# The first product of each key tile at distance 160, and the second gathered block begun one pair of heads at a time

## The chip, the cores and the metric

The kernel runs on one core of one Trainium2 chip, as one launch. The metric is the device time in microseconds (us) of that core. TensorE is called PE here, its weight loads PEld, VectorE DVE, ScalarE ACT, GpSimd POOL and SyncE SP; L199 is line 199 of the kernel before the change.

## The reference

One transformer layer on 512 tokens of width 2048, in float32:

```python
x = layer_norm(DN_ALPHA * x + hybrid_mixer(...))            # mLSTM and forgetting attention
x = layer_norm(DN_ALPHA * x + memory_cross_attention(...))
x = layer_norm(DN_ALPHA * x + peer_ffn(...))

def peer_ffn(x, w_pq, sub_keys, expert_u, expert_v):
    q = (x @ w_pq).reshape(B, S, 8, 2, 128)
    sc = jnp.einsum('bshpd,hpnd->bshpn', q, sub_keys)
    top_s, top_i = lax.top_k(sc, 16)                        # per head, on each of two halves of the key
    cand_s = top_s[..., 0, :, None] + top_s[..., 1, None, :]
    cand_i = top_i[..., 0, :, None] * 128 + top_i[..., 1, None, :]
    best_s, best_pos = lax.top_k(cand_s, 16)                # 16 of 256 pairs
    idx, g = take_along_axis(cand_i, best_pos), softmax(best_s)
    a = einsum('tkd,td->tk', expert_u[idx], x)              # 8 heads x 16 = 128 experts per token
    return einsum('tk,tkd->td', gelu(a) * g, expert_v[idx])
```

There are 16384 experts. The change touches the last of the three sublayers only, and what runs beside its beginning.

## The kernel before, in words

**Numbers.** A float32 weight is used as two halves that PE can multiply fast: `hi`, its value rounded (written by ACT, L194), and `lo`, the remainder (a subtraction on DVE, L199). The activations are split in the same way. A product of weights W and activations X is the sum of three: hi of W by hi of X, hi of W by lo of X, and lo of W by hi of X. Weights come in tiles of 1 MB (128 x 2048 numbers) by SP's DMA queue, are split into a ring of two tiles (`ring`, `shares`, L181), and are used by PE while the other ring tile is being filled. Each ring subtraction is one L199 row in the profile; the text calls it a tick.

**Blocks.** The 512 tokens are four blocks of 128. In the last sublayer blocks 0 and 1 are gathered: for each of the 128 expert places of a token, an indirect DMA on POOL's queue (L1062) fetches one row of the table `peer_u` for each of the 128 tokens, 1 MB in all, and DVE multiplies it by the token and sums (L1082, "u use"); after the gates have been applied, rows of `peer_v` are fetched and DVE adds them up (L1098, "v use"). The rows land in a pool of three buffers. Blocks 2 and 3 are dense: all 16384 experts are computed by PE, 128 key tiles of 128 experts. `next_a` (L1361) does the u part of one key tile: 16 pairs of products L1374 (hi by hi) and L1377 (hi of the weights by lo of X), then 16 products L1381 (lo by hi), 48 of 256 columns (the 256 tokens), which share a PSUM bank two tiles at a time and then go through a Gelu. `stage_o` does the v part: per tile 24 products of 512 columns (L1530, L1531, L1527).

**The choice of experts** (`Choice`, L930): PE projects the tokens to queries and multiplies by the keys (`run`, L1006) for two heads at a time, four groups; ACT copies the scores out (L1040); DVE finds the best 16 (`select`, L950, some 40 small instructions over L941 to L993). After the last group `soften` (L996) turns the scores into gates, and `indices` (L1044) makes the expert numbers, as one instruction each for all eight heads.

**Order of the work around the change.** The instructions of each engine run in the order in which a scheduler places them; the program's generators are advanced by hand. Block 0's gathers run beside the attention of the blocks after it and end at 2459.6 us. Block 1's hidden state is finished by `e1.norm`; then, in the pool `pick1`, the choice for block 1 (`cr`) is advanced step by step between the cross-attention of blocks 2 and 3 (`att`), their output projection (`res`, L789 and L270) and `e2.norm` (L802), which makes `X2`, the transposed and split activations of blocks 2 and 3. After it come, in this order: the choice for blocks 2 and 3 with 30 key tiles beside it ("top-k stage", some 2870 to 3150 us), then more key tiles while the dense gates are built (`gbuild`, to some 3440 us), a first round of v tiles without u tiles (to some 3775 us), and the main stage, in which a u tile and a v tile alternate (to some 4490 us); then the end (last sums and layer norm on DVE, then the output's DMA).

**Gathers** are paced by the ticks (`tick`, L1143): each adds `rate * cost * mult` to a credit; at 1.0 the next job's gather is issued behind that tick, and its use is put on DVE's queue `lag` ticks later. `add_jobs(1)` (L1140) puts block 1's 128 u and 128 v jobs on the list, when its choice has been made.

**Distances.** `shift` pools hold a few bytes so that the buffers after them start at another address. The "distance" of a product is the address of its moving operand (the activations) less that of its weights, modulo 256 bytes. For the key tiles it is 192 for all 16 slices of X2 before the change.

The function that makes X2 allocates its tiles from `pair(fpl, "X", 16)`: 16 tiles of 512 columns, each holding two slices, hi and lo apart.

Of the kernel before, what the change touches and what calls it, by code (L numbers as in the profile page):

```python
# [49 lines left out]
def build(tc, I, out):  # L50
    nc = tc.nc
    NC_ = PKEYS
    with ExitStack() as ctx:
# [36 lines left out]
        def parts(a, b, n):  # L90
            return [(a[:, i:i + n], b[:, i:i + n]) for i in range(0, 512, n)]
# [41 lines left out]
        iota = cp.tile([P, P], F32, tag="iota", name="iota")  # L133
        ei = [cp.tile([P, P], I32, tag=f"ei{t}", name=f"ei{t}") for t in range(2)]
        nc.gpsimd.iota(ei[0], pattern=[[1, P]], base=0, channel_multiplier=0)
# [13 lines left out]
        cols = cp.tile([P, 2, TB, 4], F32, tag="cols", name="cols")  # L149
        gg = [cp.tile([P, P], F32, tag=f"gg{t}", name=f"gg{t}") for t in range(2)]  # L150


# [622 lines left out]
        class Ends:  # L775
# [26 lines left out]
            def norm(self, i, o, alloc, dst, mid=None):  # L802
# [11 lines left out]
                for g in range(4):  # L814
# [8 lines left out]
                    for cc in range(nb):  # L823
# [15 lines left out]
                        a, l = alloc()  # L839
                        split(a, l, f)  # L840
                        o.extend(parts(a, l, w))
                        fs.append(f)
# [87 lines left out]
        class Choice:  # L930
# [74 lines left out]

            def run(self, X2, ld):  # L1006
                tp, nb = self.tp, self.nb
                for g in range(4):
# [21 lines left out]
                    for t in range(nb):  # L1030
# [10 lines left out]
                        self.select(t, 2 * g, sc)  # L1041
                self.soften()

# [16 lines left out]
        def gather(table, t, k, s):  # L1060
            rows = rows_tile("rows")
            i = nc.gpsimd.indirect_dma_start(out=rows, out_offset=None, in_=I[table],  # L1062
                                             in_offset=bass.IndirectOffsetOnAxis(ap=ei[t][:, k:k + 1], axis=0))
            pace(i, s)
            return rows
# [74 lines left out]
        def add_jobs(t):  # L1140
            jobs.extend((f, t, k) for f in (job_u, job_v) for k in range(NC_))

# [199 lines left out]
        while state["done"] < len(jobs):  # L1342
            raise RuntimeError(f"{len(jobs) - state['done']} jobs left")
        add_jobs(1)
        state["lag"] = 2
        set_rate(980.0)
        state["mult"] = 0.65
# [13 lines left out]
        def next_a(hold=None):  # L1361
# [7 lines left out]
            for uh, ul, o, w in shares(raw, 2.1, hold):  # L1369
# [8 lines left out]
                for kk in range(w // P):  # L1378
                    k = o // P + kk
                    sl = slice(kk * P, (kk + 1) * P)  # L1380
                    i = nc.tensor.matmul(bank, ul[:, sl], X2[k][0], start=False, stop=k == 15)  # L1381
            abank[1:] = [i]
# [77 lines left out]
        hs, g4 = {}, {}  # L1460
        state["mult"] = 0.86

# [203 lines left out]
```

## Time and profile before

| what | value |
|---|---|
| median of 3 runs | 4523.76 us (4520.47 to 4525.49) |
| the profiled execution | 4524.7 us |
| its span in the trace | 4523.0 us |
| mean granted PE clock | 0.992 |
| first gather of block 1 | 2869.84 us |
| last v use of block 1 ends | 4495.5 us |

The profiled execution's own time lies 1.7 us over its span and 0.9 us over the median. The span is that of the instructions in the trace; the times are of the device. On the page and in the answers of the trace, "PE busy (x)" is the time in which matmuls were under way and their number. Matmuls overlap one another, so the cost of one in a steady stream is the distance between the starts of two, not its own duration.

### The profile page before, as it was taken

Reading aid. Unit: us, or ns where it says so; the run is one execution under the profiler, and the core shown is the slowest. Engines: PE = TensorE matmul, PEld = TensorE weight load, DVE = VectorE, ACT = ScalarE, POOL = GpSimd, SP = SyncE. Lnnn points to the kernel's source line nnn. Section 1 sums busy time; section 2 is a strip of 40 time slices with the busy share of each in tenths; the row PEclk is TensorE's granted clock in tenths of the full one; section 3 lists DMA queues with packets and bytes.
Section 4 is the critical chain, followed back from the end, with each engine's and each line's share of the span. In section 5 each row is a group of like instructions: output and inputs, shape, how many; then the busy total and the mean of one; then the engine's idle time right before and its main releaser. Section 6 shows DMA issues by size and latency. Waiting matters only on the chain.

```text
span 4523.0 us, 65247 instructions
## 1 busy us (share of the span) xinstructions
PE 4414.1 (98%) x25702; PEld 3966.6 (88%) x25702; DVE 3739.9 (83%) x4326; ACT 2229.8 (49%) x3032; POOL 895.5 (20%) x631
## 2 busy tenths in 40 slices
PE   9999999999999999999999999898999999999998
PEld 8888888889888899999999778898998778999996
DVE  7877768657898977888878778899988999888888
ACT  6876776645344422333333586543773444434443
POOL 1000000000132222232222000111222223334242
PEclk9999999999999999999999999999999999999999
DMA  8899989766798889898889866786999999999997
GB/s 311 317 334 337 335 320 336 271 233 217 280 336 342 330 335 347 336 344 318 325 337 350 296 246 236 284 319 243 366 352 422 414 415 408 378 391 391 378 360 302
DMA packets 246325, 1491.85 MB, mean 330 GB/s; under 512 B 26845, under 2 KB 54557, under 8 KB 77697
## 3 DMA queue, kind: packets, MB, share of 16 engines
q1 hardware_dynamic: 151680, 890.60, 52.3%
q0 software_dynamic: 81664, 561.95, 31.7%
q10 hardware_dynamic: 12672, 35.13, 2.0%
q8 instruction: 201, 3.29, 0.3%
q14 instruction: 108, 0.88, 0.1%
HBM read 1426.72 MB, written 60.86 MB: 329 GB/s over the span
## 4 chain that ended last, share of the span: by engine, by line
PE 65%; DVE 5%; issue 4%; DMA 3%; ACT 1%; POOL 1%; DVEq 0%; ACTq 0%; SPq 0%; POOLq 0%
PE mm L220 22%; PE mm L270 6%; PE mm L263 6%; PE mm L262 6%; PE pa L1381 4%; PE mm L1530 4%; PE mm L1531 4%; PE mm L1527 4%; PE pa L1374 4%; PE pa L1377 4%; DVE ring L199 2%; DMA raw<-in_vD 1%; POOL rows L1062 1%; PE sm L638 1%; PE sm L716 1%
## 5 line engine op out<-in xcount | busy, mean ns | idle before, releaser
L194 ACT CAST ring<-raw 128x1024 fp32r<-128x1024 f32 x1568 | 1597.0, 1051 | 1456.0 <-PE mm L220 479.4
L199 DVE TENSOR_TENSOR ring<-raw,ring 128x2048 fp32r<-128x2048 f32 (+1 forms) x926 | 1813.4, 1961 | 530.0 <-ACT ring L194 268.0
L1062 POOL DMA_INDIRECT rows<-in_peer_u,ei x256 | 377.2, 1474 | 1593.0 <-DVE rows L1082 767.3
L220 PE MATMUL mm<-Ah,ring 128*128 128x384 f32 x2560 | 667.5, 339 | 1.7 <-ACT c L674 1.7
L1062 POOL DMA_INDIRECT rows<-in_peer_v,ei x256 | 451.5, 1764 | 938.0 <-DVE x2l L1098 635.1
L1098 DVE SCALAR_TENSOR_TENSOR x2l<-rows,dots,x2l 128x2048 f32<-128x2048 f32 x256 | 600.8, 2347 | 7.5 <-DMA rows<-in_peer_v,ei 7.1
L1082 DVE SCALAR_TENSOR_TENSOR rows<-rows,x2l 128x2048 f32<-128x2048 f32 x256 | 584.1, 2285 | 19.1 <-DMA rows<-in_peer_u,ei 18.9
L1374 PE MATMUL pa<-Xh,ring 128*128 128x256 f32 x2048 | 489.2, 282 | 2.9 <-ACT ring L194 2.9
L1377 PE MATMUL pa<-Xl,ring 128*128 128x256 f32 x2048 | 486.4, 280 | 0.0
L220 PEld LDWEIGHTS mm<-Ah,ring 128*128 128x128 f32 x2560 | 461.5, 188 | 7.6 <-ACT c L674 2.1
L220 PE MATMUL mm<-Al,ring 128*128 128x384 f32 x1280 | 427.0, 337 | 0.0
L1530 PE MATMUL mm<-ring,hph 128*128 128x512 f32 x1024 | 400.2, 393 | 9.0 <-ACT ring L194 6.8
L1531 PE MATMUL mm<-ring,hpl 128*128 128x512 f32 x1024 | 397.9, 390 | 0.0
L1374 PEld LDWEIGHTS pa<-Xh,ring 128*128 128x128 f32 x2048 | 387.5, 189 | 6.6 <-ACT ring L194 4.1
L1377 PEld LDWEIGHTS pa<-Xl,ring 128*128 128x128 f32 x2048 | 387.3, 189 | 2.4
L262 PE MATMUL mm<-ring,Zh 128*128 128x512 f32 x832 | 326.6, 393 | 3.3 <-ACT ring L194 3.3
L263 PE MATMUL mm<-ring,Zl 128*128 128x512 f32 x832 | 325.6, 391 | 0.0
L262 PE MATMUL mm<-ring,Ah 128*128 128x512 f32 x768 | 303.8, 396 | 1.1 <-ACT ring L194 1.1
L263 PE MATMUL mm<-ring,Al 128*128 128x512 f32 x768 | 300.5, 391 | 0.0
L1381 PE MATMUL pa<-Xh,ring 128*128 128x256 f32 x2048 | 264.4, 282 | 2.5 <-DVE ring L199 2.4
L220 PE MATMUL mm<-Bh,ring 128*128 128x384 f32 x1024 | 262.4, 339 | 3.2 <-ACT ring L194 2.5
L1527 PE MATMUL mm<-ring,hph 128*128 128x512 f32 x1024 | 254.4, 390 | 5.2 <-DVE ring L199 5.2
(395 smaller groups left out, 7042.7 us busy)
## 6 DMA issues: line engine op xcount, KB each, us to landing
raw<-in_w_in SPq DMA_DIRECT2D x256, 1024.0 KB, 6.7
raw<-in_uT SPq DMA_DIRECT2D x128, 1024.0 KB, 9.1
raw<-in_vD SPq DMA_DIRECT2D x128, 1024.0 KB, 9.5
raw<-in_w_out SPq DMA_DIRECT2D x48, 1024.0 KB, 6.1
raw<-in_peer_wq SPq DMA_DIRECT2D x48, 1024.0 KB, 5.2
raw<-in_w_xkv SPq DMA_DIRECT2D x32, 1024.0 KB, 6.5
raw<-in_w_br_ml SPq DMA_DIRECT2D x32, 1024.0 KB, 6.8
raw<-in_w_br_fx SPq DMA_DIRECT2D x32, 1024.0 KB, 7.4
```

What stands on the lines that cost most here:

```text
L194: x = nc.scalar.copy(hi[:, c:c + 1024], src[:, c:c + 1024])
L199: s = nc.vector.tensor_sub(lo, src, hi.bitcast(F32))
L220: i = nc.tensor.matmul(o, w, x, start=start and s % per == 0, stop=stop and s % per == per - 1)
L262: nc.tensor.matmul(banks[t], xh[:, tt], wh[:, c], start=k == 0, stop=False)
L263: nc.tensor.matmul(banks[t], xl[:, tt], wh[:, c], start=False, stop=False)
L1062: i = nc.gpsimd.indirect_dma_start(out=rows, out_offset=None, in_=I[table], in_offset=bass.IndirectOffsetOnAxis(ap=ei[t][:, k:k + 1], axis=0))
L1082: i = nc.vector.scalar_tensor_tensor(rows, rows, 1.0, tok[t]["x2l"], op0=ALU.mult, op1=ALU.mult, accum_out=d[:, k % GB:k % GB + 1])
L1098: i = nc.vector.scalar_tensor_tensor(acc, rows, d[:, GB + k % GB:GB + k % GB + 1], acc, op0=ALU.mult, op1=ALU.add)
L1374: i = nc.tensor.matmul(bank, uh[:, sl], xh, start=k == 0, stop=False)
L1377: nc.tensor.matmul(bank, uh[:, sl], xl, start=False, stop=False)
L1530: nc.tensor.matmul(banks[t][g], a[:, tt], vh[:, gs_], start=c == c0, stop=False)
L1531: nc.tensor.matmul(banks[t][g], b[:, tt], vh[:, gs_], start=False, stop=False)
```

## The change

**The gathers.** `settle(g)` is new: after each pair of heads has been selected, it makes the gates (an Exp on ACT; a sum, a reciprocal and a multiplication on DVE) and the indices (two instructions on DVE, into `ep[g]`) of these 32 places, and puts their 32 u jobs on the list. The ticks that follow can issue gathers at once, with `lag` 2, the same rate as before (2 x 128 / 980) and `mult` 0.6; after `e2.norm` `mult` is 0.65 as before, and `add_jobs(1)` adds the v jobs alone. In the main stage `mult` goes from 0.86 to 0.81. `soften` and `indices` no longer run for block 1.

**The distance.** The first hi tile of X2 (two slices, k = 0 and 1) moves to a pool of its own behind a shift of 224 bytes, with its halves 264 columns apart: slice 0 lies at distance 160, slice 1 at 192 like the others. In `next_a` the low products run from k = 1 to 15 first and k = 0 last. So each key tile begins and ends with a product at distance 160.

```diff
+            def settle(self, g):
+                sl = slice(32 * g, 32 * g + 32)
+                e = self.gates[:, 0, sl]
...
+                nc.scalar.activation(e, e, AF.Exp)
+                nc.vector.tensor_reduce(out=sm, in_=ev, axis=AX.X, op=ALU.add)
+                nc.vector.reciprocal(sm, sm)
+                nc.vector.tensor_tensor(gg[1][:, sl].rearrange("p (h k) -> p h k", k=16), ev,
+                                        sm.unsqueeze(2).to_broadcast([P, 2, 16]), op=ALU.mult)
...
+                nc.vector.tensor_copy(ep[g], ef)
+                jobs.extend((job_u, 1, k) for k in range(32 * g, 32 * g + 32))
...
                         self.select(t, 2 * g, sc)
-                self.soften()
+                        if settle:
+                            self.settle(g)
+                if not settle:
+                    self.soften()
...
-            jobs.extend((f, t, k) for f in (job_u, job_v) for k in range(NC_))
+            jobs.extend((f, t, k) for f in (job_u, job_v)[t:] for k in range(NC_))
...
-            cr = c.run(X2b, nc.sync)
+            state["lag"], state["rate"], state["credit"], state["mult"] = 2, 2 * NC_ / 980.0, 0.0, 0.6
+            cr = c.run(X2b, nc.sync, True)
...
             fpl = ctx.enter_context(pool("x2c", side="right"))
+            ctx.enter_context(shift("x2p0", 224, "right"))
+            xlead = ctx.enter_context(pool("x2p", side="right")).tile([P, 528], F32R, tag="X0", name="X0h")
+
+            def prX(n=[0]):
+                n[0] += 1
+                if n[0] > 1:
+                    return pair(fpl, "X", 15)
+                return xlead, fpl.tile([P, 512], F32R, tag="X", bufs=15, name=nm("Xl"))
...
-            e2.norm(1, X2, lambda: pair(fpl, "X", 16), True, mid)
+            e2.norm(1, X2, prX, True, mid)
             next(cr, 0)
-            c.indices(1)
...
-                    i = nc.tensor.matmul(bank, ul[:, sl], X2[k][0], start=False, stop=k == 15)
+                    if k:
+                        i = nc.tensor.matmul(bank, ul[:, sl], X2[k][0], start=False, stop=False)
+                i = nc.tensor.matmul(bank, ul[:, 0:P], X2[0][0], start=False, stop=True)
...
-        state["mult"] = 0.86
+        state["mult"] = 0.81
```

Where it moves instructions, first: DVE's queue in the choice for block 1, where the result of the cross-attention of blocks 2 and 3 is split for PE (`Bl`). `ring` is a tick; `eq`, `pos`, `ix` and `v` belong to the selection, `sel_g` to the gates. Before the change:

```order
L199 TENSOR_TENSOR ring_149<-raw_22343,ring_149 128x2048
L948 MAX_INDEX pos_21975<-b_21974,rep_21978 128x8
L948 MAX_INDEX pos_21975<-b_21974,rep_21984 128x8
L993 TENSOR_TENSOR sel_g_21627<-b_21974 128x32
L158 TENSOR_TENSOR Bl_22173<-sm_22167,Bh_22172 128x512
L158 TENSOR_TENSOR Bl_22182<-sm_22176,Bh_22181 128x512
L946 MATCH_REPLACE rep_22229<-v_22225,sc_22091 128x128
L976 TENSOR_SCALAR pos_21975<-pos_21975 128x32 x2
L946 MATCH_REPLACE rep_22235<-v_22225,sc_22091 128x128
L947 MAX v_22225<-rep_22229 128x8
L978 CAST pp_21990<-pos_21975 128x96
L199 TENSOR_TENSOR ring_149<-raw_22407,ring_149 128x2048
```

The same place with the change; `rows` with `x2l` (L1109) is a u use:

```order
L200 TENSOR_TENSOR ring_152<-raw_22346,ring_152 128x2048
L1109 SCALAR_TENSOR_TENSOR rows_22062,dots_21886<-rows_22062,x2l_21846 128x2048
L989 TENSOR_TENSOR pf_22014<-pp_22012 128x32
L996 TENSOR_REDUCE sel_i_2363_21628<-eq_22019 128x32
L954 MAX_INDEX ix_22273<-v_22272,rep_22276 128x8
L954 MAX_INDEX ix_22273<-v_22272,rep_22282 128x8
L1109 SCALAR_TENSOR_TENSOR rows_22132,dots_21886<-rows_22132,x2l_21846 128x2048
L159 TENSOR_TENSOR Bl_22211<-sm_22205,Bh_22210 128x512
L1109 SCALAR_TENSOR_TENSOR rows_22163,dots_21886<-rows_22163,x2l_21846 128x2048
L159 TENSOR_TENSOR Bl_22220<-sm_22214,Bh_22219 128x512
L994 TENSOR_TENSOR eq_22023<-pf_22014,iota 128x512
L952 MATCH_REPLACE rep_22288<-v_22272,sc_22125 128x128
```

Behind the tick there were small instructions only ahead of the split; now a u use, over 128 x 2048 numbers, stands behind the tick and another directly ahead of each half of the split.

Second, PE's queue where a key tile ends in the main stage (`pa` is the key tile's PSUM bank, `Xh` and `Xl` are the slices of X2, `mm` the v part's bank). Before:

```order
L1377 MATMUL pa_36874<-Xl_22753,ring_149 128x256
L1381 MATMUL pa_36874<-Xh_22620,ring_149 128x256 x2
L1381 MATMUL pa_36874<-Xh_22632,ring_149 128x256 x2
L1381 MATMUL pa_36874<-Xh_22660,ring_149 128x256 x2
L1381 MATMUL pa_36874<-Xh_22672,ring_149 128x256 x2
L1381 MATMUL pa_36874<-Xh_22700,ring_149 128x256 x2
L1381 MATMUL pa_36874<-Xh_22712,ring_149 128x256 x2
L1381 MATMUL pa_36874<-Xh_22740,ring_149 128x256 x2
L1381 MATMUL pa_36874<-Xh_22752,ring_149 128x256 x2
L1530 MATMUL mm_36645<-ring_19990,hph_36662 128x512
```

With the change; `X0h` is the tile behind the new shift:

```order
L1411 MATMUL pa_36916<-Xl_22828,ring_152 128x256
L1416 MATMUL pa_36916<-X0h,ring_152 128x256
L1416 MATMUL pa_36916<-Xh_22707,ring_152 128x256 x2
L1416 MATMUL pa_36916<-Xh_22735,ring_152 128x256 x2
L1416 MATMUL pa_36916<-Xh_22747,ring_152 128x256 x2
L1416 MATMUL pa_36916<-Xh_22775,ring_152 128x256 x2
L1416 MATMUL pa_36916<-Xh_22787,ring_152 128x256 x2
L1416 MATMUL pa_36916<-Xh_22815,ring_152 128x256 x2
L1416 MATMUL pa_36916<-Xh_22827,ring_152 128x256 x2
L1417 MATMUL pa_36916<-X0h,ring_152 128x256
L1566 MATMUL mm_36688<-ring_19993,hph_36705 128x512
```

The first low product, which read slice 0, is gone from its place (the single row of `X0h` at the beginning is slice 1) and stands last, ahead of the v part's products.

Third, DVE's queue at the end of block 1, after the last ticks (`fst` holds the sums of the layer norm, `acc` is the result of blocks 2 and 3). Before:

```order
L199 TENSOR_TENSOR ring_149<-raw_37413,ring_149 128x2048
L1098 SCALAR_TENSOR_TENSOR x2l_22923<-rows_37304,dots_30817,x2l_22923 128x2048
L1128 BN_STATS fst_37394<-x2l_22923 128x6 x4
L1129 BN_AGGR fst_37394<-fst_37394 128x2
L1110 SCALAR_TENSOR_TENSOR x2l_22923<-x2l_22923,fst_37394,lw_37332 128x1024 x2
L286 TENSOR_SCALAR fst_37394<-fst_37394 128x1
L1541 TENSOR_TENSOR acc_28987<-acc_28987,mm_37166 128x512
L1541 TENSOR_TENSOR acc_28987<-acc_28987,mm_37167 128x512
```

With the change:

```order
L1125 SCALAR_TENSOR_TENSOR x2l_21846<-rows_37280,dots_30446,x2l_21846 128x2048
L1155 BN_STATS fst_37427<-x2l_21846 128x6 x4
L1156 BN_AGGR fst_37427<-fst_37427 128x2
L1137 SCALAR_TENSOR_TENSOR x2l_21846<-x2l_21846,fst_37427,lw_37365 128x1024 x2
L287 TENSOR_SCALAR fst_37427<-fst_37427 128x1
L200 TENSOR_TENSOR ring_19993<-raw_37398,ring_19993 128x2048
...
L1140 SCALAR_TENSOR_TENSOR x2l_21846<-x2l_21846,fst_37427,lw_37367 128x1024 x2
L200 TENSOR_TENSOR ring_152<-raw_37446,ring_152 128x2048
L1577 TENSOR_TENSOR acc_29065<-acc_29065,mm_37208 128x512
L1577 TENSOR_TENSOR acc_29065<-acc_29065,mm_37209 128x512
```

Block 1's last v use and its layer norm (L1155 to L1140 on `x2l`, which are L1128 to L1113 before) now stand ahead of the last tick, and the sums of blocks 2 and 3 directly behind it; before the change all of them stood behind the last tick, and the second half of the norm (L1113 on `x2l`) stood behind the sums of blocks 2 and 3.

More of the change, by code (lines that the diff above doesn't have):

```diff
@@ L133, in build @@
         iota = cp.tile([P, P], F32, tag="iota", name="iota")
-        ei = [cp.tile([P, P], I32, tag=f"ei{t}", name=f"ei{t}") for t in range(2)]
+        ei = [cp.tile([P, P], I32, tag="ei0", name="ei0")]
         nc.gpsimd.iota(ei[0], pattern=[[1, P]], base=0, channel_multiplier=0)
@@ L150, in build @@
         gg = [cp.tile([P, P], F32, tag=f"gg{t}", name=f"gg{t}") for t in range(2)]
+        ep = [cp.tile([P, 32], I32, tag=f"ep{g}", name=f"ep{g}") for g in range(4)]
         ticks = []
@@ L839, in norm @@
                         a, l = alloc()
-                        split(a, l, f)
-                        o.extend(parts(a, l, w))
+                        if a.shape[1] == 512:
+                            split(a, l, f)
+                            o.extend(parts(a, l, w))
+                        else:
+                            av = a.rearrange("p (s c) -> p s c", s=2)[:, :, 0:w]
+                            split(av, l.rearrange("p (s c) -> p s c", s=2), f.rearrange("p (s c) -> p s c", s=2))
+                            o.extend((av[:, i], l[:, i * w:(i + 1) * w]) for i in range(2))
                         fs.append(f)
@@ L1004, in soften, with run @@
                 nc.vector.tensor_tensor(e, e, sm.unsqueeze(2).to_broadcast([P, 8 * nb, 16]), op=ALU.mult)
-            def run(self, X2, ld):
+            def settle(self, g):
+                sl = slice(32 * g, 32 * g + 32)
+                e = self.gates[:, 0, sl]
+                ev = e.rearrange("p (h k) -> p h k", k=16)
+                sm = self.tp.tile([P, 2], F32, tag="s", bufs=2, name=nm("s"))
+                nc.scalar.activation(e, e, AF.Exp)
[3 more added lines that the diff above has]
+                                        sm.unsqueeze(2).to_broadcast([P, 2, 16]), op=ALU.mult)
+                ef = self.tp.tile([P, 32], F32, tag="ef", bufs=2, name=nm("ef"))
+                nc.vector.scalar_tensor_tensor(ef, self.sel["i0"][0][:, sl], float(PKEYS), self.sel["i1"][0][:, sl],
+                                               op0=ALU.mult, op1=ALU.add)
+                nc.vector.tensor_copy(ep[g], ef)
+                jobs.extend((job_u, 1, k) for k in range(32 * g, 32 * g + 32))
+            def run(self, X2, ld, settle=False):
                 tp, nb = self.tp, self.nb
@@ L1062, in gather @@
             i = nc.gpsimd.indirect_dma_start(out=rows, out_offset=None, in_=I[table],
-                                             in_offset=bass.IndirectOffsetOnAxis(ap=ei[t][:, k:k + 1], axis=0))
+                                             in_offset=bass.IndirectOffsetOnAxis(
+                                                 ap=ep[k // 32][:, k % 32:k % 32 + 1] if t else ei[0][:, k:k + 1], axis=0))
             pace(i, s)
@@ L1314, in build @@
             c = Choice(pp, pp, 1)
-            cr = c.run(X2b, nc.sync)
+            if state["done"] < len(jobs):
+                raise RuntimeError(f"{len(jobs) - state['done']} jobs left")
+            state["lag"], state["rate"], state["credit"], state["mult"] = 2, 2 * NC_ / 980.0, 0.0, 0.6
+            cr = c.run(X2b, nc.sync, True)
             for i in range(15):
```

4 lines of the change are left out of this document (removed).

## The prediction

> **What bounds the kernel now.** The page comes first: its busy shares, then the costliest groups.
>
> ```profile
> span 4523.0 us, 65247 instructions
> PE 4414.1 (98%) x25702; PEld 3966.6 (88%) x25702; DVE 3739.9 (83%) x4326; ACT 2229.8 (49%) x3032; POOL 895.5 (20%) x631
> L199 DVE TENSOR_TENSOR ring<-raw,ring 128x2048 fp32r<-128x2048 f32 (+1 forms) x926 | 1813.4, 1961 | 530.0 <-ACT ring L194 268.0
> L1082 DVE SCALAR_TENSOR_TENSOR rows<-rows,x2l 128x2048 f32<-128x2048 f32 x256 | 584.1, 2285 | 19.1 <-DMA rows<-in_peer_u,ei 18.9
> ```
>
> PE is the engine to shorten, but 98% is a mean over stages. So I read the windows by stage next, in two tables (time, then busy time of PE, its loads, DVE, ACT and POOL, PE's clock, the DMA share and GB/s): the choice for block 1 up to X2, then everything behind it.
>
> ```profile
> 2690.00:2740.00 50.00, 46.38 (x221) 37.21 (x220) 32.57 (x34) 42.02 (x74) 0.00 (x0) 0.97 0.72 259
> 2740.00:2780.00 40.00, 40.00 (x195) 33.57 (x195) 39.42 (x114) 24.46 (x33) 0.00 (x0) 1.00 0.76 282
> 2780.00:2805.00 25.00, 25.00 (x115) 20.55 (x115) 25.00 (x79) 13.67 (x21) 0.00 (x0) 1.00 0.56 196
> 2805.00:2828.00 23.00, 23.00 (x104) 19.02 (x103) 22.21 (x45) 8.97 (x10) 0.00 (x0) 1.00 0.30 108
> 2828.00:2870.00 42.00, 29.27 (x165) 23.92 (x164) 32.62 (x100) 29.67 (x50) 0.17 (x1) 0.81 0.40 141
> ```
>
> ```profile
> 2870.00:3100.00 230.00, 229.12 (x1942) 228.71 (x1942) 213.02 (x489) 96.16 (x110) 38.83 (x27) 1.00 0.83 322
> 3345.00:3440.00 95.00, 89.94 (x756) 88.03 (x754) 74.20 (x65) 50.76 (x108) 30.03 (x14) 1.00 0.95 384
> 3440.00:3775.00 335.00, 324.65 (x1409) 259.86 (x1410) 314.65 (x271) 136.17 (x158) 84.80 (x57) 0.99 1.01 415
> 3775.00:4490.00 715.00, 711.62 (x4497) 644.95 (x4496) 627.55 (x352) 290.95 (x319) 269.41 (x123) 1.00 0.95 381
> ```
>
> Two readings matter. From 2740 to 2828 us DVE is busy 39.42 + 25.00 + 22.21 = 86.6 of 88 us, and so is PE: DVE has no room there, although nothing of PE's waits yet. And the main stage, 3775 to 4490, is PE's alone: it is busy 711.6 of 715 us, so only cheaper products shorten it.
>
> **The distance.** The steady price of a product is the step from one to the next. The timeline gives it by the rows that begin each group of 16 low products: one such row per key tile. Here are three of the stage before 3440 us and three of the one before 3100 us.
>
> ```profile
> 3412.63 1.98 PE L1381 MATMUL pa<-Xh,ring 128*128 128x256 f32 x16
> 3418.07 1.98 PE L1381 MATMUL pa<-Xh,ring 128*128 128x256 f32 x16
> 3423.51 1.98 PE L1381 MATMUL pa<-Xh,ring 128*128 128x256 f32 x16
> ```
>
> ```profile
> 2966.46 2.05 PE L1381 MATMUL pa<-Xh,ring 128*128 128x256 f32 x16
> 2972.12 2.05 PE L1381 MATMUL pa<-Xh,ring 128*128 128x256 f32 x16
> 2977.77 2.05 PE L1381 MATMUL pa<-Xh,ring 128*128 128x256 f32 x16
> ```
>
> The same 48 products cost 10.88 / 2 = 5.44 us in one place and 11.31 / 2 = 5.655 us in the other, both at a granted clock of 1.00 and at distance 192: 113.3 or 117.8 ns each. So the price is not of the instruction but of a state, and a state keeps itself over whole tiles. Which state does the main stage have? Its first two key tiles:
>
> ```profile
> 3774.05 1.98 PE L1381 MATMUL pa<-Xh,ring 128*128 128x256 f32 x16
> 3785.09 2.05 PE L1381 MATMUL pa<-Xh,ring 128*128 128x256 f32 x16
> 3796.18 2.05 PE L1381 MATMUL pa<-Xh,ring 128*128 128x256 f32 x16
> ```
>
> The first is fast, entered from the stage with waits; the second, entered behind 24 v products in an even stream, is slow, and each pair of u and v tile then takes 11.09 us. Nor does it change later: grouped from 3781 to 4435 us, the first products last 281 ns in the mean, where those of the fast tiles last 276 by the same view.
>
> ```profile
> L1374 PE MATMUL pa<-Xh,ring 128*128 128x256 f32 x944 | 225.2, 281 | 0.0
> ```
>
> 944 / 16 = 59 key tiles, each behind such a stream. If one product at another distance breaks the evenness, as a wait seems to do, those tiles cost 48 x 4.44 ns = 0.213 us less each: **59 x 0.213 = 12.6 us**, all on PE's path. No row of before has a key product at distance 160; the bounds are the two states, nothing or 12.6 us. I take the whole, because the state changes at borders between unlike products and the change puts an unlike product at each border.
>
> The Trainium skill speaks against it: "TensorE: Matmul & The Clock Gate", Part 2, the step on LDWEIGHTS, says that PE has two independent SBUF read ports, so that loading the next weights takes nothing from the running product. By that rule an address could not set the price, the sum would lack these 12.6 us, and the trace's two prices at one clock would stand unexplained; I count it below as a rival.
>
> Elsewhere a cheaper tile is worth less. In 2870 to 3100 DVE has 230 - 213 = 17 us of room; 30 key tiles there are 30 x 0.213 = 6.4 us, and the key projection's 768 products of the same shape 768 x 4.44 ns = 3.4 us. DVE's queue is in order and its selections come in bursts, so I take half of the 9.8: 5 us. In 3150 to 3440 about 18 of the tiles are slow by the same rows of the timeline, 3.8 us, beside DVE and DMA limits (DMA share 0.95): 2 us. In 3440 to 3775 there are no key tiles.
>
> **The early gathers.** With the change the u uses of block 1 begin when the first pair of heads is settled. The two POOL rows on either side of the gap show what was idle until then:
>
> ```profile
> 2459.59 1.01 POOL L1062 DMA_INDIRECT rows<-in_peer_v,ei  x1 [9.02 <-DVE x2l L1098]
> 2869.84 2.74 POOL L1062 DMA_INDIRECT rows<-in_peer_u,ei  x1 [409.24 <-DMA x2d<-r]
> ```
>
> DVE's order in the changed kernel has 11 u uses before the ticks at which X2's last input is added (2833 us), where there were none. At 2.285 us they are 25.1 us. The three settles there add five small instructions each; the nearest rows of block 1's own are
>
> ```profile
> 2858.18 0.29 DVE L1002 TENSOR_REDUCE s<-sel_g 128x8 f32<-128x128 f32 x1 [0.97 <-ACT sel_g L1001]
> 2859.69 0.20 DVE L1003 RECIPROCAL s<-s 128x8 f32<-128x8 f32 x1
> 2860.35 0.28 DVE L1004 TENSOR_TENSOR sel_g<-sel_g,s 128x128 f32<-128x128 f32 x1
> 2864.18 0.29 DVE L1046 SCALAR_TENSOR_TENSOR ef<-sel_i,sel_i 128x128 f32<-128x128 f32 x1
> 2864.51 0.23 DVE L1048 CAST ei<-ef 128x128 int32<-128x128 f32 x1
> ```
>
> 1.3 us for all eight heads, and on a quarter of the columns at most 0.9 us: 3 x 0.9 = 2.7. Together **27.8 us of new work in a stretch where DVE is full**. Behind it in DVE's queue stand the ticks and both halves of the split `Bl`, for which PE waits (L270, L262), and so X2. What takes some of it up? DVE's idle time around the stretch:
>
> ```profile
> 2743.13 0.87 DVE L941 MAX8 v<-sc 128x8 f32<-128x128 f32 x4 [0.58 <-ACT sc L1040]
> 2845.68 0.87 DVE L941 MAX8 v<-sc 128x8 f32<-128x128 f32 x4 [5.50 <-ACT sc L1040]
> PE mm L270 <- DVE ring L199: 6.8, 2, 4.7
> ```
>
> The changed order starts the first selection one or two ticks earlier, in the window 2690 to 2740 where DVE idles 17 us: some 5 us. The 5.5 us ahead of the last selection can be filled too, and about 1 us of small gaps. The last row (PE waits from 2690 to 2870) says that before the change the ring already ran late at the end, 6.8 us in two waits, so there is no lead left that could hide more. 27.8 - 11.5 = **16 us later**; the ends are 27.8 with no cover, and 8 if the selection starts twice as early and the rest of X2's norm, where DVE idles 42 - 32.6 = 9.4 us, takes the surplus.
>
> Is it paid back? Block 1's gathers are then 12 to 15 uses ahead. From 2870 to 3150 the order places 30 of them in both kernels, in 3440 to 3775 as many as before, and only in the last third of the main stage fewer per tick (0.87 for 1.0, the lower `mult`). There PE hardly waits for DVE:
>
> ```profile
> PE pa L1381 <- DVE ring L199: 2.4, 7, 0.4
> PE mm L1527 <- DVE ring L199: 1.0, 1, 1.0
> ```
>
> That is at most 3.4 us; I take 2. The lead is therefore given back only at the end, where it lets block 1's norm leave the tail:
>
> ```profile
> 4493.16 2.35 DVE L1098 SCALAR_TENSOR_TENSOR x2l<-rows,dots,x2l 128x2048 f32<-128x2048 f32 x1
> 4499.42 1.97 PE L1527 MATMUL mm<-ring,hph 128*128 128x512 f32 x8
> 4500.81 2.47 DVE L1541 TENSOR_TENSOR acc<-acc,mm 128x512 f32<-128x512 f32 x4
> 4511.15 2.48 DVE L1113 SCALAR_TENSOR_TENSOR x2l<-x2l,fst,lw 128x1024 f32<-128x1024 f32 x2
> 4516.90 2.48 DVE L1113 SCALAR_TENSOR_TENSOR acc<-acc,fst,lw 128x1024 f32<-128x1024 f32 x2
> ```
>
> PE ends at 4501.4, DVE at 4519.4. Gone from between is the 2.48 of `x2l`, and the first sums and half of the statistics need no longer wait until 4500.8: some 1.5 us. **4 us less** (3 to 6). POOL, SP and ACT keep their counts and are not the bound: POOL is busy 269 of 715 us in the main stage, and the early gathers meet a DMA share of 0.30 to 0.76.
>
> **The sum**, against the profiled 4524.7: -12.6 - 5 - 2 for the distance, +16 for DVE's full stretch, -2 and -4 later: -9.6, or 4515.1. The profiled run is 0.9 over the median, so on the median's scale **4514 us**. Its own range goes from all cheap (8 for the push, 12.6 + 9.8 + 3.8 = 26.2 for the distance, 3.4 and 6: -28) to 27.8 - 12.6 - 3 = +12.
>
> **The rivals.** *The distance does nothing, the full queue decides* (slower). The v stream sets the slow state in all 59 tiles whatever came before, which speaks for it; one product of 48 is little, and the other 15 low products sit at 192 as ever. Then X2 comes 16 us later through DVE's queue, and 2 and 4 come back: +10, **4534 us**, from -1 to +25 (8 - 6 - 3 and 27.8 - 3). It decides as soon as the uses ahead of X2 cost over 6 us, that is three of the 11. I give it 0.3; the rule on the two ports above belongs here. *The gathers do not act so early* (no change). A use is placed by the order, but if DVE's part runs under PE's work, because selections and ticks have slack that the windows do not show, the push is nearer 8 than 16; with the distance doing nothing that is +2, **4525 us**. The 86.6 of 88 us speaks against it: 0.1. *My case*, the cheaper state in the main stage: 0.6. For it speaks that fast tiles occur in runs, entered after broken streams; against it that no row shows what starts a run.
>
> **How the numbers follow.** 0.2% is 9 us, about what a measurement of this kernel can tell from no change. My case at -9.6 lies at that border with an uncertainty of some 9 either way: of its 0.6, 0.35 is faster by more, 0.22 within and 0.03 slower. The first rival: 0.03 faster, 0.1 within, 0.17 slower. The second: 0.02, 0.07, 0.01. Together 0.40, 0.39 and 0.21. The range reaches from the better half of my case, -22 (4502), to four past the first rival's own value, 4538.
>
> **What would show it.** In the changed profile: rows of the low products in the main stage of 1.86 us for 15 instead of 2.05 for 16, and pairs 10.88 us apart instead of 11.09. The end of the first v round, 3775 us before, comes later by about 16 less what the tiles before it gave (9 us); if it comes earlier than before, the push was wrong. The first POOL gather of block 1 falls near 2770 us; waits of PE for L200 and for the split grow between 2770 and 2870 by 10 to 25 us. PE's end to DVE's end shrinks from 18 to 14 us. I am wrong in the mechanism if the main pairs still lie 11.09 apart and the time has nevertheless fallen, or if they lie 10.88 apart and it has not.

## The result and the profile after

The changed kernel took 4551.62 us (median of 4 runs, 4548.36 to 4554.67) against 4523.74: a ratio of 1.0063 with a 95% interval of 1.0051 to 1.0075, 28 us slower. Forecast were 4514 us and a range up to 4538. The page after, span and busy shares:

```profile
span 4549.9 us, 65269 instructions
PE 4413.5 (97%) x25702; PEld 3959.7 (87%) x25702; DVE 3742.2 (82%) x4340; ACT 2231.9 (49%) x3037; POOL 883.4 (19%) x631
```

PE's busy time is 0.6 us less than before and the span 26.9 us more: the loss is waiting. To see where, I set the ticks side by side. Both kernels have 926, so tick 620 means the same work in both; the table gives the lateness of the changed kernel in us, worked out from the starts of the ring subtractions in the two traces.

```
tick                       620   641   642   655   796   916   925   PE's last product   end of span
before, starts at       2674.7 2768.7 2772.1 2867.3 3775.0 4443.0 4491.0        4501.0        4523.0
changed kernel later by    3.7  15.0  29.1  38.5  33.1  25.8  36.0          30.0          26.9
```

The 3.7 us ahead of tick 620 are in work that the change does not touch; other profiles below differ there by up to 7 us either way. Two things happen behind it: from tick 620 to 655 (which ends X2) the changed kernel loses 34.8 us, and in the main stage (796 to 916) it gains 7.3. The end then gives nothing back: from tick 916 to PE's last product 4.2 us are lost, and 3.1 saved in the tail.

The loss, by the changed kernel's windows over the stretch; the columns are as before (PE, its loads, DVE, ACT, POOL, clock, DMA share, GB/s):

```profile
2730.00:2780.00 50.00, 42.48 (x195) 33.10 (x194) 42.06 (x120) 24.41 (x30) 1.11 (x2) 1.00 0.69 246
2780.00:2845.00 65.00, 55.10 (x230) 44.28 (x229) 61.44 (x127) 25.21 (x38) 12.00 (x9) 0.89 0.80 300
2845.00:2910.00 65.00, 45.76 (x233) 37.04 (x232) 54.14 (x132) 39.89 (x60) 4.82 (x3) 0.82 0.63 224
```

In the first window PE already idles 7.5 of 50 us, and DVE is not full. But the first early gather comes only at the end of that window. The rows of POOL's timeline:

```profile
2778.59 0.94 POOL L1088 DMA_INDIRECT rows<-in_peer_u,ep  x1 [314.20 <-DVE v L953]
2779.83 2.88 POOL L1088 DMA_INDIRECT rows<-in_peer_u,ep  x1 [0.30 <-ACT ring L195]
2783.01 0.94 POOL L1088 DMA_INDIRECT rows<-in_peer_u,ep  x1 [0.30 <-issue]
```

So 10.6 us were lost by tick 639, which starts at 2774.3 us in the changed kernel, before any early gather had been issued. Who waited? ACT's waits for loads between 2674 and 2910, of the changed kernel:

```profile
ACT ring L195 <- DMA raw<-in_peer_wq: 25.9, 9, 4.9
ACT ring L195 <- DMA raw<-Bd: 22.2, 5, 10.4
ACT ring L195 <- DMA raw<-Ad: 2.7, 2, 1.4
```

and of the kernel before, all that there are:

```profile
ACT ring L194 <- DMA raw<-Bd: 1.0, 1, 1.0
```

The weights come late. The reason stands in a function that the change does not touch, `load_raw`:

```python
            raws["idle"] = raws["idle"] + 1 if jobs and state["done"] >= len(jobs) else 0
            if raws["idle"] > 6 and raws["n"] % 2:
                raw = rows_tile("raw")
            ...
```

Once all gather jobs on the list have been issued, and six loads later, every other weight load uses one of the gathers' three row buffers; with a job still open all loads share two. The first `settle` ends that loan. Counted in the two programs, 40 loads go into row buffers before and 28 after: the 12 that are missing are those between the first settled pair and the end of X2.

The second piece is the jump of 14 us at tick 642. DVE's queue there:

```profile
2786.21 2.28 DVE L1109 SCALAR_TENSOR_TENSOR rows<-rows,x2l 128x2048 f32<-128x2048 f32 x1
2790.68 2.29 DVE L1109 SCALAR_TENSOR_TENSOR rows<-rows,x2l 128x2048 f32<-128x2048 f32 x1 [1.99 <-DMA rows<-in_peer_u,ep]
2795.55 2.29 DVE L1109 SCALAR_TENSOR_TENSOR rows<-rows,x2l 128x2048 f32<-128x2048 f32 x1 [1.57 <-DMA rows<-in_peer_u,ep]
2797.77 1.28 DVE L867 TENSOR_REDUCE xst<-mm 128x2 f32<-128x512 f32 x2
2801.23 2.27 DVE L200 TENSOR_TENSOR ring<-raw,ring 128x2048 fp32r<-128x2048 f32 x1
```

Three u uses, two of which wait for their rows to land, stand ahead of the softmax of the cross-attention (L867) and of the next tick.

The gain, by the low products of two key tiles of the main stage, 14 of one name in a row each:

```profile
3864.42 1.75 PE L1416 MATMUL pa<-Xh,ring 128*128 128x256 f32 x14
3875.36 1.75 PE L1416 MATMUL pa<-Xh,ring 128*128 128x256 f32 x14
```

13 steps take 1.75 - 0.276 = 1.47 us, 113.4 ns each, and a pair of u and v tile 10.94 us for 11.09 before: the distance does act.

### The profile page after: what moved, and what is told of

Its sections match the earlier page's. It is cut to its first block, busy times and chain, and to the rows that moved or that the text cites. A ratio compares the mean times of both kernels' runs of the same rounds, so it can differ in the third digit from the quotient of the medians.

```text
span 4549.9 us, 65269 instructions
## 1 busy us (share of the span) xinstructions
PE 4413.5 (97%) x25702; PEld 3959.7 (87%) x25702; DVE 3742.2 (82%) x4340; ACT 2231.9 (49%) x3037; POOL 883.4 (19%) x631
## 4 chain that ended last, share of the span: by engine, by line
PE 63%; DVE 6%; DMA 5%; issue 4%; ACT 2%; POOL 0%; ACTq 0%; DVEq 0%; POOLq 0%; SPq 0%
PE mm L221 22%; PE mm L271 5%; PE mm L263 5%; PE mm L264 5%; PE pa L1408 4%; PE pa L1411 4%; PE pa L1416 4%; PE mm L1566 3%; PE mm L1567 3%; PE mm L1563 3%; DVE ring L200 3%; DMA raw<-in_vD 1%; DMA rows<-in_peer_v,ep 1%; ACT ring L195 1%; DVE rows L1109 1%
## 5 line engine op out<-in xcount | busy, mean ns | idle before, releaser
L200 DVE TENSOR_TENSOR ring<-raw,ring 128x2048 fp32r<-128x2048 f32 (+1 forms) x926 | 1811.2, 1960 | 548.1 <-ACT ring L195 294.4
L1109 DVE SCALAR_TENSOR_TENSOR rows<-rows,x2l 128x2048 f32<-128x2048 f32 x256 | 583.3, 2282 | 18.7 <-DMA rows<-in_peer_u,ei 9.9
L1408 PE MATMUL pa<-Xh,ring 128*128 128x256 f32 x1792 | 420.6, 278 | 0.0
L1566 PE MATMUL mm<-ring,hph 128*128 128x512 f32 x1024 | 400.8, 393 | 6.7 <-ACT ring L195 5.0
L1088 POOL DMA_INDIRECT rows<-in_peer_u,ep x128 | 190.7, 1490 | 1036.9 <-DVE rows L1109 406.3
L1088 POOL DMA_INDIRECT rows<-in_peer_v,ep x128 | 275.5, 2153 | 536.9 <-DVE x2l L1125 297.7
L1408 PEld LDWEIGHTS pa<-Xh,ring 128*128 128x128 f32 x1792 | 337.9, 189 | 0.3
L1088 POOL DMA_INDIRECT rows<-in_peer_u,ei x128 | 174.3, 1362 | 517.7 <-DVE rows L1109 315.3
L1088 POOL DMA_INDIRECT rows<-in_peer_v,ei x128 | 176.2, 1376 | 471.0 <-DVE x2l L1125 254.0
```

The lines of the kernel that those rows point to most:

```text
L200: s = nc.vector.tensor_sub(lo, src, hi.bitcast(F32))
L1109: i = nc.vector.scalar_tensor_tensor(rows, rows, 1.0, tok[t]["x2l"], op0=ALU.mult, op1=ALU.mult, accum_out=d[:, k % GB:k % GB + 1])
L1408: i = nc.tensor.matmul(bank, uh[:, sl], xh, start=k == 0, stop=False)
L1566: nc.tensor.matmul(banks[t][g], a[:, tt], vh[:, gs_], start=c == c0, stop=False)
```

## The experiments

Theory A says that the loss has several parts ahead of X2 (late loads, u uses, what they wait for), and that the distance saves in the main stage alone. Rivals: B, the u uses in DVE's queue are all of the loss; C, the gain in the main stage comes from the lower rate of gathers; others are named where they come up. The kernel before was run again beside each of three groups of experiments: medians 4524.48 us (20 runs), 4525.03 (21) and 4524.47 (35), from 4515.35 to 4534.23 in all. Each ratio is to its own group and has a 95% interval. All stretches and prices below are read from one profiled execution of each kernel.

**The two halves of the change.** First the distance by itself: `before` with the new tile for X2's first slices and the new order of the low products.

```diff
-            e2.norm(1, X2, lambda: pair(fpl, "X", 16), True, mid)
+            e2.norm(1, X2, prX, True, mid)
...
-                    i = nc.tensor.matmul(bank, ul[:, sl], X2[k][0], start=False, stop=k == 15)
+                    if k:
+                        i = nc.tensor.matmul(bank, ul[:, sl], X2[k][0], start=False, stop=False)
+                i = nc.tensor.matmul(bank, ul[:, 0:P], X2[0][0], start=False, stop=True)
```

> The kernel before with the first tile of X2 at distance 160 and the low products of slice 0 last; gathers as before. Theory A (the distance saves in the main stage and nowhere else, as the changed kernel's ticks 796 to 916 show, 9 us): 4515 us, from 4511 to 4518, and between ticks 630 and 655 no difference from before. Rival C (those 9 us come from the lower rate of gathers in the main stage, the distance does nothing): 4524, within 3 of before.

Measured: 4516.08 us, ratio 0.9981 (0.9971 to 0.9990). Then the other half, the changed kernel with these three edits undone:

> The changed kernel with X2 and the order of the low products as before. Theory A: the whole loss stays and the distance's 9 us are missing: 4561 us, from 4556 to 4566. Rival C: as the changed kernel, 4552.

Measured: 4559.41 us, ratio 1.0072 (1.0054 to 1.0090). Both as A said: -8.4 and +34.9 us, in sum 26.5, where the whole change cost 27.9. In the main stage the gathers alone, with the lower `mult`, keep the old price, 11.09 us per pair:

```profile
3870.58 2.05 PE L1401 MATMUL pa<-Xh,ring 128*128 128x256 f32 x16
3881.67 2.05 PE L1401 MATMUL pa<-Xh,ring 128*128 128x256 f32 x16
```

It gains 0.6 us between ticks 796 and 916, where the changed kernel gains 7.3, so rival C is out. The loss before X2 is the gathers' alone: 35.2 us between ticks 620 and 655 here, 0.3 in the run of the distance alone.

**What the loss is made of.** The measure for the next runs is this stretch, from the start of tick 620 to that of tick 655: 192.6 us before, 227.4 in the changed kernel. In the runs in which nothing there should differ (the distance alone, and four further below) it came out at 192.4 to 192.9, so differences of a microsecond mean something. First, `before` without the loan of the row buffers:

```diff
-            if raws["idle"] > 6 and raws["n"] % 2:
+            if raws["idle"] > 6 and raws["n"] % 2 and not raws.get("held"):
...
                         self.select(t, 2 * g, sc)
+                        if self.nb == 1 and not self.lean:
+                            raws["held"] = True
```

> The kernel before, but from the first selection of block 1's choice on no weight load goes to the gathers' three row buffers, as in the changed kernel (12 loads fewer); no gather, no settle, no distance. Theory A (a part of the loss is that loads have two buffers alone and come late; in the changed kernel 12 us had been lost before its first gather was issued): 12 us slower, 4536, from 4531 to 4548, with waits of ACT for the loads of in_peer_wq and Bd. Rival B (the u uses in DVE's queue make all of the loss): 4524, within 4 of before.

Measured: 4530.27 us, ratio 1.0014 (1.0004 to 1.0025), 5.8 us slower, and 203.2 us in the stretch:

```profile
2677.96 2.27 DVE L199 TENSOR_TENSOR ring<-raw,ring 128x2048 fp32r<-128x2048 f32 x1
2881.12 2.29 DVE L199 TENSOR_TENSOR ring<-raw,ring 128x2048 fp32r<-128x2048 f32 x1 [1.25 <-ACT ring L194]
```

Here no gather, no settle and no distance has changed, and ACT waits for the loads as in the changed kernel (23.6 us for `in_peer_wq`, 21.4 for `Bd`). 10.6 us of the stretch are the loan; rival B falls. The median moved by less than A said and lies just under its range. The profiled execution was the slowest of its ten (4539.79 us), so 10.6 may be high for the usual one; but in all six traces in which the loads have two buffers of their own and no others, 11.3 to 12.8 us are lost between ticks 620 and 641.

Next the length of the uses. In the changed kernel the early ones are cut to 64 columns; the edit below is by a flag that is set until X2 is done.

```diff
-                i = nc.vector.scalar_tensor_tensor(rows, rows, 1.0, tok[t]["x2l"], op0=ALU.mult, op1=ALU.mult,
+                n = 64 if early else D
+                i = nc.vector.scalar_tensor_tensor(rows[:, :n], rows[:, :n], 1.0, tok[t]["x2l"][:, :n], op0=ALU.mult, op1=ALU.mult,
...
```

> The changed kernel, in which the first 96 or so u uses (those whose gather is issued before X2 is done, and no others) multiply and sum 64 columns of 2048 and leave the rest out, so they cost DVE almost nothing. Theory A: the uses are about half of the loss, the late loads stay: 4552 - 20 = 4532 us, from 4525 to 4538. Rival B: the whole 35 us before X2 go, 4517, from 4513 to 4522.

The number of uses in that text is wrong: 12 are cut, since 12 gathers are issued there. Measured: 4546.37 us, ratio 1.0054 (1.0035 to 1.0073); 214.6 us in the stretch, 12.8 less than the changed kernel. Both misjudged it: the length of the uses is a third of the loss, less than A's half. 22.0 us stay, and the loan explains half of these.

What is the rest? The same kernel, but the 12 short uses read the token instead of the rows, so that DVE never waits for a gather:

```diff
+                x = tok[t]["x2l"][:, :n]
+                y = gat["pool"].tile([P, 64], F32, tag="dummy", name=nm("dummy")) if early else rows
+                i = nc.vector.scalar_tensor_tensor(y[:, :n], x if early else rows, 1.0, x, op0=ALU.mult, op1=ALU.mult,
...
```

> As the run with short early uses, but the 12 early uses read 64 columns of the token alone and not the gathered rows, so DVE's queue does not wait for a gather to land; the gathers still go and the loads still have two buffers (the u sums of these 12 places are left out). Between ticks 620 and 655 the changed kernel loses 35 us, the short uses 22, two load buffers alone 11. Theory A (the rest, 11 us, is DVE's queue standing still until the third gather has landed, with the softmax behind it): 22 - 10 = 12 us lost there, from 9 to 15. Rival D (the gathers' own traffic delays the weight loads, landing is not waited for): 20 to 23.

Measured: 4542.11 us, ratio 1.0036 (1.0021 to 1.0051), and 209.8 us in the stretch, 17.2 over before. Neither end: the landing is worth 4.8 us, half of what A gave it, and 6.6 stay beside the loan. So the traffic was tried next, the same kernel without the 12 gathers themselves:

```diff
-            rows = gather("peer_u", t, k, s)
+            rows = None if early else gather("peer_u", t, k, s)
```

> As the run with short early uses that don't read the rows, but the 12 early gathers are not issued either; two load buffers and the order of DVE's queue stay (the u sums of 12 places are left out). That run lost 17 us between ticks 620 and 655, two load buffers alone 11. Theory D (the other 6 us are the gathers' 12 MB on the DMA engines, which make the late loads later): 11 us there, from 9 to 13. Rival H (they come from the small instructions' places in the queues): 16 to 18.

Measured: 4535.93 us, ratio 1.0027 (1.0017 to 1.0038), and 204.9 us in the stretch:

```profile
2672.61 2.27 DVE L200 TENSOR_TENSOR ring<-raw,ring 128x2048 fp32r<-128x2048 f32 x1
2877.56 2.29 DVE L200 TENSOR_TENSOR ring<-raw,ring 128x2048 fp32r<-128x2048 f32 x1 [1.34 <-ACT ring L195]
```

As theory D of that text said: 4.9 us are the gathers' traffic beside loads that are late already. The remaining pieces, the settles and the order, are 12.3 - 10.6 = 1.7. That settling by itself is free is shown by the changed kernel with the jobs put on the list behind X2:

```diff
-                jobs.extend((job_u, 1, k) for k in range(32 * g, 32 * g + 32))
...
-            jobs.extend((f, t, k) for f in (job_u, job_v)[t:] for k in range(NC_))
+            jobs.extend((f, t, k) for f in (job_u, job_v) for k in range(NC_))
```

> The changed kernel with the gates and indices still made per pair of heads and the distance kept, but the u jobs put on the list behind X2 as before, at the rates of before. Theory A (settling costs 15 small DVE instructions ahead of X2 and nothing else): 1 to 4 us between ticks 620 and 655, and the distance's 8 us stay: 4518, from 4514 to 4521. Rival: settling is itself a main part of the loss: over 8 us there, 4525 or more.

Measured: 4517.11 us, ratio 0.9979 (0.9968 to 0.9991), 192.7 us in the stretch: 0.1 us for settling, less than A's 1 to 4. (Its `mult` in the main stage is 0.86, as before.)

The staircase, each step one run, in us between ticks 620 and 655 over before:

```
10.6   two load buffers alone
12.3   with settles, the order and 12 empty uses                 +1.7
17.2   with the 12 gathers issued, their rows not waited for     +4.9
22.0   with the uses waiting for the rows                        +4.8
34.8   with the uses at full length: the changed kernel         +12.8
```

The sizes hold for this order of taking things away. By the same traces the jump of 14 us at tick 642 is the gathers' own, not the length of the uses: 13.5 are left with short uses, 9.2 when no row is waited for and 2.1 without gathers. The length is paid behind it, up to tick 655.

The staircase is of this stretch only. The whole times fall in the same order, but in other steps: the changed kernel is 27.9 us over its own runs of before, the short uses 21.9, those that wait for no rows 17.1 and those without gathers 11.5. From tick 655 to 796 these profiles move against before by anything from -5.4 us (the changed kernel) to +10.7 (short uses); why was not taken apart.

Can the loan be kept? The changed kernel with the row buffers taken in turn by loads and early gathers (the flag `keep` is set until X2 is done):

```diff
-            raws["idle"] = raws["idle"] + 1 if jobs and state["done"] >= len(jobs) else 0
+            raws["idle"] = raws["idle"] + 1 if jobs and state["done"] >= len(jobs) or raws.get("keep") else 0
```

> The changed kernel, in which weight loads go on taking the gathers' row buffers in turn with the early gathers until X2 is done. Theory A (11 of the 35 us are the two load buffers): 24 us lost between ticks 620 and 655, from 20 to 30, 4541 in all. Rival D (gathers and loads then wait for each other's buffers, and what DVE waits for comes later still): 35 or more.

Measured: 4575.76 us, ratio 1.0105 (1.0085 to 1.0124), 55.7 us lost in the stretch. A missed; rival D had it. PE's waits there:

```profile
PE mm L263 <- ACT ring L195: 26.9, 8, 10.7
PE mm L271 <- DVE ring L200: 17.0, 7, 6.5
```

A weight load now waits for a buffer that a gather holds until its use: SP's queue waits 23.1 us for two u uses there, which it does not do in the changed kernel. The use in its turn stands behind ticks that need weights. Shared in this way, the three buffers do not serve both.

**What the distance does.** The order of the low products without the distance:

> The kernel before with the low products of slice 0 last in each key tile and all distances at 192. Theory A (the distance of the first product makes the cheaper state): main stage as before, 11.09 us per pair, 4524 within 3. Rival E (the break in the order of slices makes it): 8 us faster, 4516.

Measured: 4525.22 us, ratio 1.0001 (0.9992 to 1.0011); pairs of 11.10 us in the main stage:

```profile
3862.31 1.93 PE L1382 MATMUL pa<-Xh,ring 128*128 128x256 f32 x15
3873.41 1.93 PE L1382 MATMUL pa<-Xh,ring 128*128 128x256 f32 x15
```

The order does nothing. The distance without the order (`prX` as above, `next_a` as before):

> The kernel before with the first tile of X2 at distance 160 and the low products in their old order, so a key tile begins at 160, but does not end there. Theory A1 (the first product of a tile behind the v stream sets the state for the tile): as the distance with the order, main pairs of 10.88 us, 4516, from 4512 to 4519. Rival F (what the tile ends with, ahead of the v stream, matters as well, or the one low product at 160 in the middle turns it back): pairs near 11.0 or 11.09, 4520 to 4525.

Measured: 4512.91 us, ratio 0.9976 (0.9967 to 0.9985), the fastest of all; pairs of 10.92 us:

```profile
3863.90 1.75 PE L1395 MATMUL pa<-Xh,ring 128*128 128x256 f32 x14
3874.82 1.75 PE L1395 MATMUL pa<-Xh,ring 128*128 128x256 f32 x14
```

A1 holds: the product at 160 at the beginning is enough, without the one at the end (slice 0 also gives the 33rd product of each tile here). And all of X2 at 160, by another shift:

```diff
-            ctx.enter_context(shift("x2c0", 64, "right"))
+            ctx.enter_context(shift("x2c0", 96, "right"))
```

> The kernel before with all of X2 32 bytes lower, so that every key product is at distance 160, none unlike its neighbours. Theory A1 (it is the entry from the v stream that matters, and 160 is a good entry): main pairs of 10.88 us, 4516, from 4512 to 4519. Rival G (the first product must be unlike those behind it): 11.09 per pair, 4524 within 3; or a third price altogether if the distance sets the price product by product.

Measured: 4533.05 us, ratio 1.0021 (1.0011 to 1.0030), pairs of 11.16 us:

```profile
3884.66 2.06 PE L1381 MATMUL pa<-Xh,ring 128*128 128x256 f32 x16
3895.82 2.06 PE L1381 MATMUL pa<-Xh,ring 128*128 128x256 f32 x16
```

A1's 4516 failed here. 160 is no good distance in itself: the key tiles of the main stage are at a third, higher price (11.16 is 0.07 over 11.09 for 48 products), as G's last branch allows. But the price does not go product by product, since in the lead alone 46 of 48 products are at 192 as before and cost less. A first product at 160 pays when the rest is at 192; whether any other unlike distance would do was not tried. The steps from product to product in the main stage, medians over 58 tiles by the starts in the traces, show how it goes:

```
                          first products of a tile     later ones    first v products behind it
before                    117 118 118 117 118          117-118 ns    227 227 227 227 227
distance alone            117 124 116 114 113          113-114 ns    233 233 236 224 231
lead alone                117 125 116 114 113          113 ns        232 232 231 227 227
all at 160                117 119 119 118 124          116-122 ns    236 232 231 227 226
```

One product at 160 is followed by a step of 124 or 125 ns instead of 118, and after two more the stream runs at 113. The first v products behind such a tile are mostly 4 to 9 ns dearer. That is not the price of a cheap tile alone, since three of them are as dear behind the dear tiles of all at 160. Of the estimated 0.213 us per tile 0.146 are left (11.093 - 10.947).

Not every tile gets it. In the changed kernel 13 of the 60 key tiles of the main stage are broken in two by 8 or 16 products of the v part, and what stands behind the break begins with a slice at 192. One such place, to be compared with the 14 low products at 3864.42 us:

```profile
4434.26 1.99 PE L1563 MATMUL mm<-ring,hph 128*128 128x512 f32 x8
4438.09 1.81 PE L1416 MATMUL pa<-Xh,ring 128*128 128x256 f32 x14
```

The 13 steps are 118 ns each here. In all 13 tiles the 16 or 32 products behind the break are back at the old price, and in the lead alone three such rests that begin at 192 are, while the one that begins with slice 0 at 160 costs 113 ns. By 320 products at 4.4 ns more, an estimate from these steps, the breaks cost 1.4 of the 8.8 us that 60 tiles at 0.146 would bring. The entry is not the whole rule: in four kernels with all at 192, seven of nine rests of 16 low products were cheap behind such a break, and the first key tile of the changed kernel's main stage was dear although it begins at 160.

**The end.** Is the shorter tail to be had with the distance alone, if block 1's norm is spread between the last ticks by a higher rate of gathers?

```diff
-        state["mult"] = 0.86
+        state["mult"] = 0.90
```

> The distance alone, gathers begun behind X2 as before, with the main stage's mult at 0.90 in place of 0.86, so that block 1's norm lies between the last four ticks. Theory A2 (the changed kernel's shorter tail, 3 us, was paid for with PE's wait for the last ticks, which stood directly behind the norm; spread out it is free): 3 us under the distance alone, 4513, from 4510 to 4516. Rival: the faster gathers make DMA or DVE late in the main stage or PE waits at the end as before: 4516 to 4521.

Measured: 4516.21 us, ratio 0.9982 (0.9973 to 0.9991), as the distance alone (4516.08). A2 failed: from tick 916 to PE's last product this run loses 3.3 us (the distance alone: none), and the tail is 3.1 us shorter. With the earlier norm, PE waits more for the last ticks (this run's waits from 4440 us on):

```profile
PE mm L1543 <- DVE ring L199: 2.7, 4, 1.0
PE mm L1546 <- ACT ring L194: 0.3, 1, 0.3
```

## Why the prediction was wrong, point by point

- **The distance, main stage: right in the mechanism, too large.** Forecast -12.6; the changed kernel gained 7.3 between ticks 796 and 916, and the distance alone 6.8 to PE's last product. The price fell for most of the products in 52 of 60 tiles (57 with the distance alone), but the entry products and the first v products took back a third of the 0.213 us, and the broken tiles some more. That an unlike product at the border sets the state is borne out by the lead alone and by all at 160; it is needed at the tile's beginning only, and it is not the whole rule. Read as the prediction read it, the Trainium skill's "TensorE: Matmul & The Clock Gate", Part 2, the step on LDWEIGHTS (two independent SBUF read ports), would have made all of these distances equal. Here 113.3, 117.8 and some 119 ns stand at a granted clock of 1.00 for the same product, so for this kernel the measurement decides against reading it that way. Why an address has this effect was not tried.
- **The distance elsewhere: -5 and -2 forecast, next to nothing found.** The distance alone gained 2.0 us in the top-k stage (ticks 655 to 700) and lost 1.1 from there to 796. In the run with the order alone 24 of 30 tiles of the top-k stage happened to be fast, which would be 5 us of PE's work, and the stage ended 0.6 us earlier against before. So PE does not set the pace there; that DVE does is argued from its 213 busy us of 230, not tried.
- **The early gathers: the step that failed is "+16 for DVE's full stretch".** The uses' own part came near (12.8 measured in the stretch for their length, 16 taken for uses and settles after 11.5 of cover; the pieces of that cover were not tried). What failed was what went with it, that the early gathers "meet a DMA share of 0.30 to 0.76" and so cost nothing else. They took the row buffers from the weight loads (10.6), their traffic made the late loads later (4.9), and DVE's queue stood still for their rows (4.8). 34.8 came, above my bound of 27.8, which was worked out on DVE alone. The rows of 2790 and 2795 us show DVE's queue waiting in its order, with a softmax and a tick behind two uses that wait. This agrees with the Trainium skill, "TensorE: Matmul & The Clock Gate", "Architectural detail", which calls that queue strict FIFO.
- **The low DMA share was read wrongly.** From 2780 to 2828 us before it was 0.56 and 0.30; I took that as room. It was low because the loads had run far ahead into three more buffers. Without the loan (`before` with two load buffers) the share is lower at first and higher then, 0.52 and 0.57 in place of 0.72 and 0.76, then 0.58 and 0.56 in place of 0.56 and 0.30:

```profile
2690.00:2740.00 50.00, 46.53 (x223) 37.26 (x222) 29.95 (x32) 37.63 (x70) 0.00 (x0) 0.97 0.52 193
2740.00:2780.00 40.00, 33.68 (x138) 24.65 (x137) 35.99 (x108) 21.48 (x26) 0.00 (x0) 0.91 0.57 210
2780.00:2805.00 25.00, 22.54 (x105) 17.54 (x103) 23.40 (x64) 15.06 (x27) 0.00 (x0) 1.00 0.58 204
2805.00:2828.00 23.00, 23.00 (x101) 19.06 (x102) 22.71 (x58) 8.92 (x9) 0.00 (x0) 1.00 0.56 190
```

Free bandwidth is no free buffer.

- **The tail: 3.1 us less, forecast 4, but 4.2 more ahead of it.** The norm's 7.7 us of DVE moved in front of the last ticks, and PE waits for these, 3.1 us on L200 from 4440 us on where it waited 1.0 before. The rise of 2.1 is half of the 4.2; the other half was not placed. The run with `mult` 0.90 shows the same trade.
- **The waits of the main stage: -2 forecast.** They went from 3.4 us before to 2.5, about 1.
- **The rival that came nearest** was the first one in its sign and place, the queue ahead of X2, but with the distance acting; its price of +10 had the same gap in it. By the prediction's own last sign, pairs near 10.88 us and no fall in the time, the mechanism as a whole was wrong: the pairs came to 10.94 and the time rose.

By measured terms: +3.7 ahead of tick 620, +34.8 to X2, -5.4 from there to tick 796, -7.3 in the main stage, +4.2 at PE's end, -3.1 in the tail: 26.9, the difference of the spans. The -5.4 were not taken apart; 4.2 of them lie between ticks 780 and 796, where the run with the gathers alone gained 3.4, so the distance has little part in them.

## What to carry to other kernels

Before work is moved into a quiet stretch, ask what the idle resource is lent to: a pool of buffers that stands empty on one list may be the prefetch depth of another, and the code that lends it is nowhere near the change. Early work in an in-order queue costs its wait for its inputs as well as its own time, to everything behind it, and its transfers compete with those that are late already. And two edits in one change should be timed apart: here one was worth -8 to -12 us and the other +35.

## What the runs showed of the hardware

A product's price depended on the address of its moving operand; the weights' addresses stayed where they were, so whether the difference of the two counts, as the word distance has it, is not shown. In the main stage, behind v products, 256 columns cost 117.8 ns each with all at distance 192, some 119 with all at 160, and 113.3 when a tile at 192 was entered by one product at 160 (with a step of 124 ns behind it). The state then lasted until the end of the tile or until v products broke into it, over 44 and more products, and the first v products behind it were dearer too. Key tiles without a v stream between them do not follow this: in the top-k stage 0 of 30 were fast before, 30 of 30 in the run of the lead alone, 24 with the order alone, 5 in the changed kernel; what decides it there stays open.
